# Opening two of the four PSUM results of each seven-product pair with a ScalarE copy and a VectorE sum

## The chip, the cores and the metric

The kernel runs on one core of a Trainium2 chip. The metric is the device time of one execution in microseconds (us). Engines are named as in the profile: PE is TensorE (PEld its weight loads), DVE is VectorE, ACT is ScalarE, POOL is GpSimd, SP is SyncE, which only issues DMAs here.

## The reference

A decoder of two layers on 256 positions (SEQ) of width 2048 in fp32: a mixer (attention and a gated recurrence between an input and an output projection), a SwiGLU feed-forward net (FFN), and a gated embedding per layer (PLE). The parts that the change touches are the last products of each block:

```python
mix = jnp.concatenate([attn, hgrn], axis=-1) @ w_out          # 2048 -> 2048
ffn = (jax.nn.silu(h @ w_ffn_gate) * (h @ w_ffn_up)) @ w_ffn_down   # 2048 -> 5632 -> 2048
ple = jax.nn.sigmoid(h @ w_ple_gate) * (p @ w_ple_proj)       # gate: 2048 -> 2048
```

Residuals and RMS norms lie between them (the names `mix`, `ffn`, `ple` and `h` stand in for the reference's functions).

## The kernel before

Weights stream from HBM in slabs 512 columns wide (W); one DMA of 512 KB brings 256 rows of the depth. Every fp32 weight tile `wr` is split in two: ScalarE casts the high half `wh` (L307), VectorE makes the low half `wl` = `wr` - `wh` (L317). Activations are held split and transposed in the tiles `ck`. A block product is then three matmuls into the same PSUM bank: high by high, low by high, high by low. They are L420, L423 and L424 in `paired`, and L332, L333 and L335 in `strip`, which does the columns that aren't paired. One bank holds 128 positions by 512 columns, so a strip of 512 columns needs two banks, t = 0 and t = 1.

`paired` handles two strips of 512 columns at once. Most of the depth is done plainly (`plain`): results e and a are t = 0 and 1 of the first strip (`wa`), c and d are t = 0 and 1 of the second (`wb`). On the first 512 rows of the depth (256 per block) the 2 by 2 block product is done with seven block products instead of eight (`fast`), and with `half` also on half of the next 512 rows. For this, sums of activation blocks (`sum`, from `mixed`) are made beforehand, and differences of weight blocks (`sub`, L436) on VectorE. An eighth quantity, u, is summed in a bank of another pool (tile name `ms`), in three steps:

- u's first products; they are a part of e. ScalarE copies u to SBUF (`saved`, L429; the first entry of `x`).
- after c's first products, p5 = a copy of c (L429 again); then e's and a's first products.
- `second` adds products to u and copies it again (for c, the first entry of `y`).
- `third` adds to c, adds to u a last time, copies it (for a), and adds u to p5 on VectorE (L498; that sum is for d).

At the end of each result, `summed` adds the saved tile to the bank on VectorE (L397) and hands the sum to the caller. The FFN's down projection does the addition itself: L1258 in the first group of hidden columns (bank plus saved tile into `macc`), L1260 and L1262 in the later ones (bank, then saved tile, onto `macc`).

There are 19 paired calls in a layer: two in the output projection `w_out` (the second with t = 1 running SKEW slabs behind t = 0), ten with `half` for gate and up of the FFN (a in gate's columns, c and d in up's), six in `w_ffn_down` (of which three a layer with `mixed_order`, which interleaves the strips), one in `w_ple_gate`. With two layers that is 38.

The pool `pacc` has four banks for e, a, c and d; u's pool has four too. The code calls the engines in a program order; Tile's scheduler then orders each engine's queue by its own cost model and puts the semaphore waits in. Every engine works its queue in order. Callers matter at three places: `merged` (L1187) after `w_out`, where a sum of squares (L201, ScalarE) and a product with the gain (L1187, VectorE) read each result, followed by the norm L559 and the transposes on PE (L227); `gated`, where ScalarE's L1210 (Silu) and VectorE's L1217 read results; and `gate_of` (L1302 to L1304), the PLE gate, which also ends the program.

Of the kernel before, what the change touches and what calls it, by code (L numbers as in the profile page):

```python
# [12 lines left out]
ALU = mybir.AluOpType  # L13
# [34 lines left out]
def decoder(ctx: ExitStack, tc: tile.TileContext, x, p, positions, w_in, attn_sinks,  # L48
# [16 lines left out]
    V, S, G, T = nc.vector, nc.scalar, nc.gpsimd, nc.tensor  # L65
# [29 lines left out]
    def tick():  # L95
        clock[0] += 1
        for gen in list(running):
            if next(gen, True):
                running.remove(gen)
        for item in [q for q in queue if q[0] <= clock[0]]:  # L100
            queue.remove(item)
            item[1]()

    def nat(shape=(P, W), dt=F32):
        return np_.tile(list(shape), dt, tag="nat", name="nat")

    def bank(shape=(P, W)):
        return pms.tile(list(shape), F32, tag="ms", name="ms")
# [44 lines left out]
    ps = bank()  # L153
# [49 lines left out]
    def split(src, hi, lo):  # L203

        a = S.copy(hi, src)  # L205
        v = V.tensor_tensor(lo, src, hi.bitcast(F32), op=ALU.subtract)  # L206
        return a, v
# [102 lines left out]
    def load_w(w, c, col, raw=None, hi=None):  # L310

        if raw is None:
            raw = fetch_w(w, c, col)
        if hi is None:
            hi = high(raw)
        lo = wps.tile([P, 2, W], F32R, tag="wl", name="wl")
        marks["lo"] = V.tensor_tensor(lo, raw, hi.bitcast(F32), op=ALU.subtract)  # L317
        return hi, lo
# [75 lines left out]
    def summed(done):  # L394

        def both(t, ps, x):
            V.tensor_tensor(x, ps, x, op=ALU.add)  # L397
            done(t, x)
        return both

    def paired(lhs, sums, wa, wb, cols, done_a, done_b, nch=8, row0=0, skews=(0, 0),
               after=None, mixed_order=False, half=None):

        base = row0 // (2 * P)
        opened = {}

        def psum(name):
            return pacc.tile([P, W], F32, tag="acc", name=name)

        def block(c, t):  # L410
            def get(k):
                kt = 2 * c + k
                return tuple(a[:, kt % 4, t * P:(t + 1) * P] for a in lhs[kt // 4])
            return get

        def acc(ps, x, hl, ks=(0, 1)):
            hi, lo = hl
            for k in ks:
                xh, xl = x(k)
                T.matmul(ps, xh, hi[:, k], start=id(ps) not in opened, stop=False,  # L420
                         skip_group_check=True)
                opened[id(ps)] = ps
                T.matmul(ps, xl, hi[:, k], start=False, stop=False, skip_group_check=True)  # L423
                marks["pe"] = T.matmul(ps, xh, lo[:, k], start=False, stop=k == ks[-1],  # L424
                                       skip_group_check=True)

        def saved(ps):
            b = nat()
            S.copy(b, ps)  # L429
            return b  # L430

        def parts(r):
            return load_w(None, 0, 0, raw=r)

        def sub(dst, p, q):
            V.tensor_tensor(dst, p, q, op=ALU.subtract)  # L436

        def split_one(r, k):
            hi = wps.tile([P, 2, W], F32R, tag="wh", name="wh")
            lo = wps.tile([P, 2, W], F32R, tag="wl", name="wl")  # L440
            split(r[:, k], hi[:, k], lo[:, k])
            return hi, lo

        def fast():
            mix = sums()
            r11, r12 = fetch_w(wa, base, cols[0]), fetch_w(wb, base, cols[1])
            if half:
                more = half()
                g, p = fetch_w(wa, base + 2, cols[0]), fetch_w(wb, base + 2, cols[1])
            r21, r22 = fetch_w(wa, base + 1, cols[0]), fetch_w(wb, base + 1, cols[1])  # L450
            u = bank()
            acc(u, block(0, 0), parts(r11))
            if half:
                gx = parts(g)
                acc(u, block(2, 0), gx, (0,))
            x = [saved(u)]
            sub(r11, r12, r11)
            c = psum("accc")
            acc(c, mix(1), parts(r11))
            if half:  # L460
                sub(g[:, 0], p[:, 0], g[:, 0])
                acc(c, more(1), split_one(g, 0), (0,))
            p5 = saved(c)
            tick()
            e = psum("acce")
            acc(e, block(1, 0), parts(r21))
            if half:
                acc(e, block(2, 0), gx, (1,))
            sub(r11, r22, r11)
            sub(r21, r21, r11)  # L470
            a = psum("acca")
            acc(a, block(1, 1), parts(r21))
            if half:
                sub(g[:, 0], p[:, 1], g[:, 0])
                sub(g[:, 1], g[:, 1], g[:, 0])
                g24 = parts(g)
                acc(a, block(2, 1), g24, (1,))
                sub(p[:, 0], p[:, 1], p[:, 0])
            tick()
            sub(r12, r22, r12)  # L480
            y = []

            def second():
                acc(u, mix(2), parts(r11))
                if half:
                    acc(u, more(2), g24, (0,))
                y.append(saved(u))

            def third():
                acc(c, mix(4), parts(r22))  # L490
                if half:
                    p32 = parts(p)
                    acc(c, more(4), p32, (1,))
                acc(u, mix(3), parts(r12))
                if half:
                    acc(u, more(3), p32, (0,))
                x.append(saved(u))
                V.tensor_tensor(p5, u, p5, op=ALU.add)  # L498
                y.append(p5)
                tick()  # L500
            return e, a, c, x, y, second, third

        head = 3 if half else 2

        def plain(w, col, banks, skew, end, c0=head, c1=nch, then=None):
            n = c1 - c0
            ws = {}
            for i in range(n + skew):
                if i < n:
                    ws[i] = load_w(w, base + c0 + i, col)  # L510
                    acc(banks[0], block(c0 + i, 0), ws[i])
                    if i == n - 1 and end:
                        end(0)
                if i >= skew:
                    acc(banks[1], block(c0 + i - skew, 1), ws[i - skew])
                if then and i == 0:
                    then()
                tick()
            if end:
                end(1)  # L520

        e, a, c, x1, x2, second, third = fast()

        def end_a(t):
            done_a(t, (e, a)[t], x1[t])

        def end_b(t):
            done_b(t, (c, d)[t], x2[t])
        if mixed_order:
            plain(wa, cols[0], (e, a), 0, None, c1=nch - 2, then=second)  # L530
            third()
            d = psum("accd")
            plain(wb, cols[1], (c, d), 0, None, c1=nch - 2)
            plain(wa, cols[0], (e, a), 0, end_a, c0=nch - 2)
            plain(wb, cols[1], (c, d), 0, end_b, c0=nch - 2)
            return
        def then():
            second()
            if after:
                after[0]()  # L540
        plain(wa, cols[0], (e, a), skews[0], lambda t: t or end_a(t), then=then)
        third()
        end_a(1)
        if after:
            after[1]()
        d = psum("accd")
        plain(wb, cols[1], (c, d), skews[1], end_b)

    def load_gain(g, col):
# [210 lines left out]
    for l in range(DEPTH):  # L760
# [473 lines left out]
        for gi, glen in enumerate(FF_GROUPS):  # L1234
# [11 lines left out]
            for s in range(4):  # L1246
# [5 lines left out]
                def done(t, ps, x, s=s, gB=gB if last else None):  # L1252
                    m = macc[s][:, t]
                    if gi == 0:
                        if x is None:
                            S.copy(m, ps)
                        else:
                            V.tensor_tensor(m, ps, x, op=ALU.add)  # L1258
                        return
                    V.tensor_tensor(m, ps, m, op=ALU.add)  # L1260
                    if x is not None:
                        V.tensor_tensor(m, x, m, op=ALU.add)  # L1262
                    if last:
                        square_sum(m, ssf[t][:, s:s + 1])
                        V.tensor_tensor(m, m, gB, op=ALU.mult)
                        if s == 3:
                            post_norm(macc, ssf, t, nss, nxT, gain_cols(64, l, 16), (4, 3)[t])
# [96 lines left out]
```

## Time and profile before

| | |
|---|---|
| runs of the kernel | 2342.43, 2343.69, 2344.05 us (median 2343.69) |
| profiled execution | 2343.71 us, its span 2342.0 us |
| granted TensorE clock, mean | 0.998 |
| products of 512 columns in `paired`: one group, L420 on e | x456, 177.9 us by the records, 390 ns each |
| casts L307 | x974, 1005.2 us, mean 1054 ns |
| low halves L317 | x974, 1160.1 us, mean 1222 ns |
| additions L397 on e, a, c, d | 26 each, 682 to 688 ns |
| HBM read and written | 474.57 and 29.36 MB, 215 GB/s over the span |

Matmuls are pipelined: their records overlap, and the time from start to start is what a product costs. In the lists of single instructions an entry is start, length, engine, line, operation, output and inputs, and in brackets the idle time before it and what ended it. In the groups (instructions of one line and form) come the count, the busy time, the mean, and the idle time before them.

### The profile page before, as it was taken

To read this page: it belongs to the slowest core of one execution; us is meant where nothing else is said; L and a number is where in the kernel's file an instruction comes from. 1 tells how busy PE (TensorE), PEld (TensorE's weight loads), DVE (VectorE), ACT (ScalarE), POOL (GpSimd) and SP (SyncE) were. 2 spreads that over 40 slices of the span, in tenths; PEclk is the share of its full clock that TensorE was granted. 3 is DMA by queue.
4 is the path that set the end of the run, shared out by engine and by line. 5 is a ranking of instruction groups with operands and counts; after the bars stand their busy time and mean duration, and the time that the engine had idled before them with its cause. 6 is when DMAs were issued, how large, how long until landed. Compare 5 with 4: busy or idle time off the path is not lost.

```text
span 2342.0 us, 33183 instructions
## 1 busy us (share of the span) xinstructions
PE 2326.9 (99%) x11731; PEld 1914.5 (82%) x11731; DVE 1971.1 (84%) x2535; ACT 1412.5 (60%) x2050; POOL 114.7 (5%) x229
## 2 busy tenths in 40 slices
PE   9999999999999999999999999999999999999999
PEld 7888888888888888888788888888888888888887
DVE  7786878898998999888767868788989989988885
ACT  6576557565656566657556665566656556565564
POOL 4100001000000000002010000010000000000010
PEclk9999999999999999999999999999999999999999
DMA  8666467576557565766776674676757575676743
GB/s 294 221 212 214 150 233 253 175 248 214 202 203 257 200 234 189 276 217 201 228 219 216 205 232 138 225 241 197 262 170 240 206 255 180 215 236 231 256 162 135
DMA packets 301671, 506.14 MB, mean 216 GB/s; under 512 B 23712, under 2 KB 69696, under 8 KB 301504
## 3 DMA queue, kind: packets, MB, share of 16 engines
q1 hardware_dynamic: 301200, 503.93, 64.6%
q8 instruction: 92, 1.51, 0.3%
q14 instruction: 75, 0.61, 0.1%
q0 software_dynamic: 64, 0.02, 0.0%
q10 hardware_dynamic: 240, 0.07, 0.0%
HBM read 474.57 MB, written 29.36 MB: 215 GB/s over the span
## 4 chain that ended last, share of the span: by engine, by line
PE 91%; DVE 4%; DMA 2%; issue 1%; ACT 1%; POOL 1%; SPq 0%; DVEq 0%; ACTq 0%; POOLq 0%
PE acc L332 10%; PE acc L335 10%; PE acc L333 10%; PE accc L420 5%; PE accc L423 5%; PE accc L424 5%; PE acce L420 4%; PE acca L420 4%; PE acce L423 4%; PE acca L423 4%; PE acce L424 4%; PE acca L424 4%; PE accd L424 3%; PE accd L420 3%; PE accd L423 3%; PE ms L420 3%
## 5 line engine op out<-in xcount | busy, mean ns | idle before, releaser
L307 ACT CAST wh<-wr 128x1024 fp32r<-128x1024 f32 x974 | 1005.2, 1054 | 726.5 <-DVE wr L436 208.5
L317 DVE TENSOR_TENSOR wl<-wr,wh 128x1024 fp32r<-128x1024 f32 x974 | 1160.1, 1222 | 242.3 <-ACT wh L307 230.5
L332 PE MATMUL acc<-wh,ck 128*128 128x512 f32 x1120 | 442.4, 395 | 0.7 <-ACT ck L205 0.7
L335 PE MATMUL acc<-wl,ck 128*128 128x512 f32 x1120 | 436.6, 391 | 0.8 <-DVE wl L317 0.8
L333 PE MATMUL acc<-wh,ck 128*128 128x512 f32 x1120 | 437.1, 391 | 0.1
L335 PEld LDWEIGHTS acc<-wl,ck 128*128 128x128 f32 x1120 | 210.2, 188 | 45.9 <-DVE wl L317 2.0
L332 PEld LDWEIGHTS acc<-wh,ck 128*128 128x128 f32 x1120 | 210.2, 188 | 44.0 <-ACT ck L205 0.9
L333 PEld LDWEIGHTS acc<-wh,ck 128*128 128x128 f32 x1120 | 210.4, 188 | 42.2 <-DVE ck L206 0.5
L436 DVE TENSOR_TENSOR wr<-wr 128x1024 f32<-128x1024 f32 (+1 forms) x232 | 235.5, 1039 | 1.2
L420 PE MATMUL acce<-wh,ck 128*128 128x512 f32 x456 | 177.9, 390 | 0.0
L424 PE MATMUL acce<-wl,ck 128*128 128x512 f32 x456 | 177.4, 389 | 0.0
L420 PE MATMUL acca<-wh,ck 128*128 128x512 f32 x456 | 177.4, 389 | 0.0
L423 PE MATMUL acce<-wh,ck 128*128 128x512 f32 x456 | 177.4, 389 | 0.0
L424 PE MATMUL acca<-wl,ck 128*128 128x512 f32 x456 | 177.4, 389 | 0.0
L423 PE MATMUL acca<-wh,ck 128*128 128x512 f32 x456 | 177.4, 389 | 0.0
L424 PE MATMUL accd<-wl,ck 128*128 128x512 f32 x360 | 141.6, 393 | 0.2
L420 PE MATMUL accd<-wh,ck 128*128 128x512 f32 x360 | 140.5, 390 | 0.0
L423 PE MATMUL accd<-wh,ck 128*128 128x512 f32 x360 | 140.1, 389 | 0.0
L423 PE MATMUL accc<-wh,ck 128*128 128x512 f32 x360 | 140.1, 389 | 0.0
L420 PE MATMUL accc<-wh,ck 128*128 128x512 f32 x360 | 140.0, 389 | 0.0
L424 PE MATMUL accc<-wl,ck 128*128 128x512 f32 x360 | 140.0, 389 | 0.0
L420 PEld LDWEIGHTS acce<-wh,ck 128*128 128x128 f32 x456 | 85.7, 188 | 18.0 <-ACT ck L205 0.3
(278 smaller groups left out, 3211.9 us busy)
## 6 DMA issues: line engine op xcount, KB each, us to landing
wr<-in_w_in_dram SPq DMA_DIRECT2D x176, 512.0 KB, 4.6
wr<-in_w_ffn_gate_dram SPq DMA_DIRECT2D x176, 512.0 KB, 5.9
wr<-in_w_ffn_up_dram SPq DMA_DIRECT2D x176, 512.0 KB, 6.1
wr<-in_w_ffn_down_dram SPq DMA_DIRECT2D x176, 512.0 KB, 7.3
wr<-in_w_out_dram SPq DMA_DIRECT2D x64, 512.0 KB, 5.0
wr<-in_w_ple_gate_dram SPq DMA_DIRECT2D x64, 512.0 KB, 5.0
turn<-nat SPq DMA_DIRECT2D x86, 256.0 KB, 2.5
nat<-turn SPq DMA_DIRECT2D x344, 64.0 KB, 3.6
```

The costliest lines, as they stand in the source:

```text
L307: marks["hi"] = S.copy(hi, raw)
L317: marks["lo"] = V.tensor_tensor(lo, raw, hi.bitcast(F32), op=ALU.subtract)
L332: T.matmul(ps[t], xh, hi[:, k], start=first, stop=False)
L333: T.matmul(ps[t], xl, hi[:, k], start=False, stop=False)
L335: marks[t, c] = marks["pe"] = T.matmul(ps[t], xh, lo[:, k], start=False, stop=last)
L420: T.matmul(ps, xh, hi[:, k], start=id(ps) not in opened, stop=False, skip_group_check=True)
L423: T.matmul(ps, xl, hi[:, k], start=False, stop=False, skip_group_check=True)
L424: marks["pe"] = T.matmul(ps, xh, lo[:, k], start=False, stop=k == ks[-1], skip_group_check=True)
L436: V.tensor_tensor(dst, p, q, op=ALU.subtract)
```

## The change

u's first copy goes to PSUM: ScalarE copies u into bank e (`moved`) and marks the bank as opened, so that e's first product accumulates on it. In `third`, VectorE's sum of u and p5 goes into bank d, and d's first product accumulates on that. For e and d nothing is left to add at the end, so `summed` hands the bank on, and the callers read PSUM there. a and c stay as they were. In the down projection the first group copies bank e and bank d to `macc` on ScalarE, a branch that was there for `strip`; the later groups leave L1262 out. Bank c is taken from the pool ahead of e.

```diff
     def summed(done):
         def both(t, ps, x):
+            if x is None:
+                done(t, ps)
+                return
             V.tensor_tensor(x, ps, x, op=ALU.add)
             done(t, x)
...
+        def moved(dst, src):
+            S.copy(dst, src)
+            opened[id(dst)] = dst
+            return dst
...
-            x = [saved(u)]
+            c = psum("accc")
+            e = moved(psum("acce"), u)
+            x = [None]
             sub(r11, r12, r11)
-            c = psum("accc")
             acc(c, mix(1), parts(r11))
...
             p5 = saved(c)
             tick()
-            e = psum("acce")
             acc(e, block(1, 0), parts(r21))
...
                 x.append(saved(u))
-                V.tensor_tensor(p5, u, p5, op=ALU.add)
-                y.append(p5)
+                d = psum("accd")
+                V.tensor_tensor(d, u, p5, op=ALU.add)
+                opened[id(d)] = d
+                y.append(None)
                 tick()
+                return d
...
-            third()
-            d = psum("accd")
+            d = third()
             plain(wb, cols[1], (c, d), 0, None, c1=nch - 2)
...
-        third()
+        d = third()
         end_a(1)
         if after:
             after[1]()
-        d = psum("accd")
         plain(wb, cols[1], (c, d), skews[1], end_b)
```

The lines below the edit move by up to 9: L420, L423 and L424 become L423, L426 and L427, L429 becomes L437, L397 becomes L400; the new copy is L431, and the sum L498 is now L507 with a bank as its output. The number of matmuls stays the same.

What moves in the queues shows at three places. PE, first gate/up pair, where u's third step ends (`ms`) and d begins, before:

```order
L424 MATMUL ms_4442<-wl_4646,sum_4243 128x512
L420 MATMUL accc_4463<-wh_4673,ck_3211 128x512
L423 MATMUL accc_4463<-wh_4673,ck_3212 128x512
L424 MATMUL accc_4463<-wl_4675,ck_3211 128x512
L420 MATMUL accc_4463<-wh_4673,ck_3211 128x512
L423 MATMUL accc_4463<-wh_4673,ck_3212 128x512
L424 MATMUL accc_4463<-wl_4675,ck_3211 128x512
L420 MATMUL accd_4670<-wh_4673,ck_3211 128x512
```

The same place on PE with the change:

```order
L427 MATMUL ms_4436<-wl_4638,sum_4237 128x512
L423 MATMUL accc_4454<-wh_4665,ck_3211 128x512
L426 MATMUL accc_4454<-wh_4665,ck_3212 128x512
L427 MATMUL accc_4454<-wl_4667,ck_3211 128x512
L423 MATMUL accc_4454<-wh_4665,ck_3211 128x512
L426 MATMUL accc_4454<-wh_4665,ck_3212 128x512
L427 MATMUL accc_4454<-wl_4667,ck_3211 128x512
L423 MATMUL accc_4454<-wh_4683,ck_3213 128x512
L426 MATMUL accc_4454<-wh_4683,ck_3214 128x512
L427 MATMUL accc_4454<-wl_4685,ck_3213 128x512
L423 MATMUL accc_4454<-wh_4683,ck_3213 128x512
L423 MATMUL accd_4658<-wh_4665,ck_3211 128x512
```

Between u's last product and d's first one there were six products on c, and now there are ten. In the last pair of each group of hidden columns there are seven instead of six.

ScalarE, PLE pair of layer 0, where the first copy of u was (`nat_10507`) and where p5 is copied (`nat_10521`), before:

```order
L307 CAST wh_10593<-wr_10591 128x1024
L307 CAST wh_10631<-wr_10629 128x1024
L201 ACTIVATE junk_10617,ssx0_9959<-x_9648 128x512
L1302 ACTIVATE nat_10481<-acc1_10313,rp1_10267 128x512
L307 CAST wh_10649<-wr_10647 128x1024
L307 CAST wh_10667<-wr_10665 128x1024
L307 CAST wh_10685<-wr_10683 128x1024
L201 ACTIVATE junk_10627,ssx1_9960<-x_9650 128x512
L429 COPY nat_10507<-ms_10496 128x512
L429 COPY nat_10521<-accc_10510 128x512
```

The same place on ScalarE with the change (`acce_10456` is bank e, `nat_10469` is p5):

```order
L307 CAST wh_10540<-wr_10538 128x1024
L431 COPY acce_10456<-ms_10444 128x512
L307 CAST wh_10578<-wr_10576 128x1024
L201 ACTIVATE junk_10564,ssx0_9907<-x_9596 128x512
L1311 ACTIVATE nat_10429<-acc1_10261,rp1_10215 128x512
L307 CAST wh_10596<-wr_10594 128x1024
L307 CAST wh_10614<-wr_10612 128x1024
L307 CAST wh_10632<-wr_10630 128x1024
L201 ACTIVATE junk_10574,ssx1_9908<-x_9598 128x512
L437 COPY nat_10469<-accc_10455 128x512
```

The first copy of u has moved ahead of four casts and both sums of squares; the copy of p5 has stayed behind them.

ScalarE, second pair of the output projection in layer 0, before:

```order
L201 ACTIVATE junk_3564,ssm0_3205<-nat_3309 128x512
L307 CAST wh_3691<-wr_3689 128x1024
L201 ACTIVATE junk_3574,ssm1_3206<-nat_3254 128x512
L429 COPY nat_3600<-ms_3589 128x512
L429 COPY nat_3614<-accc_3603 128x512
```

And with the change:

```order
L201 ACTIVATE junk_3562,ssm0_3205<-nat_3308 128x512
L307 CAST wh_3687<-wr_3685 128x1024
L201 ACTIVATE junk_3571,ssm1_3206<-accd_3452 128x512
L431 COPY acce_3598<-ms_3586 128x512
L307 CAST wh_3705<-wr_3703 128x1024
```

Here the copy of u has kept its place behind a cast and a sum of squares; the sum of squares before it now reads bank d of the first pair, and p5's copy has moved one cast back.

In the FFN's gate and up pairs the sum into bank d (L507) stands, as L498 did, behind the first low half of the next pair on VectorE; with the last pair of a group no low half is ahead of it.

## The prediction

> **What bounds the kernel now.** I read the shares of the page first, then the list of waits of PE, then the timeline at each place where PE stood still.
>
> ```profile
> span 2342.0 us, 33183 instructions
> ...
> PE 2326.9 (99%) x11731; PEld 1914.5 (82%) x11731; DVE 1971.1 (84%) x2535; ACT 1412.5 (60%) x2050; POOL 114.7 (5%) x229
> ```
>
> TensorE is busy all the time, and VectorE's 84% and ScalarE's 60% are no bound as such. A "busy" PE says little, so the question is how regularly its products start. Here are the last product of a partial sum u and the first product on bank d in a gate/up pair, with six products on bank c between (list of single instructions: start, length, engine, line, output and inputs):
>
> ```profile
> 449.68 0.39 PE L424 MATMUL ms<-wl,sum 128*128 128x512 f32 x1
> ...
> 451.26 0.39 PE L420 MATMUL accd<-wh,ck 128*128 128x512 f32 x1
> ```
>
> Seven starts lie 1.58 us apart, so a product costs 0.226 us although its record is 0.39 us long. The number of products doesn't change, so only stops between them, and the last few microseconds, can move the time. PE's own list of waits (total us, times, longest) is short:
>
> ```profile
> PE ms L420 <- ACT nat L429: 2.0, 1, 2.0
> PE ms L227 <- DVE x L559: 1.9, 4, 0.8
> ...
> PE acc L335 <- DVE wl L317: 0.8, 2, 0.4
> ...
> PE ms L215 <- DMA x<-in_x_dram: 0.2, 1, 0.2
> ```
>
> A weight transfer isn't in it; the one DMA is the load of x at the start. So SP's slightly changed order of loads is hidden behind PE, and I count it at nothing; one load that came too late would cost its own wait once, and there is no row to size it by. VectorE's 76 saved additions (two of four in each of 38 pairs) shorten nothing by being gone: they lie beside PE. They count only where PE waits behind one of them.
>
> **What the change removes.** Three places.
>
> (1) The PLE gate of layer 0. PE stops for a PSUM bank of u that ScalarE hasn't copied out yet:
>
> ```profile
> 1134.52 0.39 PE L332 MATMUL ms<-wh,pT 128*128 128x512 f32 x1
> 1136.94 0.79 PE L420 MATMUL ms<-wh,sum 128*128 128x512 f32 x1 [2.04 <-ACT nat L429]
> ```
> ```profile
> 1132.43 2.93 ACT L307 CAST wh<-wr 128x1024 fp32r<-128x1024 f32 x3
> 1135.70 0.63 ACT L201 ACTIVATE junk<-x 128x512 f32<-128x512 f32 x1 [0.33 <-ACT wh L307]
> ...
> 1136.33 0.57 ACT L429 COPY nat<-ms 128x512 f32<-128x512 f32 x1
> ```
>
> The copy isn't needed early, so it stands behind three casts and a sum of squares. The pitch is 2.42 us, 2.19 too long. After it PE runs at half clock (stretches: bounds, length, busy time and instructions of PE, PEld, DVE, ACT, POOL, then granted clock):
>
> ```profile
> 1134.00:1136.90 2.90, 0.90 (x4) 0.40 (x3) 2.90 (x4) 2.57 (x6) 0.00 (x0) 1.00 0.70 210
> 1136.90:1140.40 3.50, 3.46 (x8) 2.78 (x9) 2.52 (x3) 2.34 (x3) 0.00 (x0) 0.51 0.97 324
> ...
> 380.00:388.00 8.00, 6.84 (x34) 5.05 (x34) 7.19 (x15) 7.57 (x24) 3.99 (x8) 1.00 0.75 244
> ```
>
> Eight products take 3.50 us instead of 8 x 0.226 = 1.81, another 1.69. With the change, e's first product needs u's copy, and the copy stands ahead of four casts and both sums of squares in ScalarE's queue. Both go: 2.19 + 1.69 = **-3.9 us**. In layer 1 there is no such row (the list has it once).
>
> (2) The end of the output projection, once a layer:
>
> ```profile
> 381.88 0.39 PE L333 MATMUL acc<-wh,ck 128*128 128x512 f32 x1
> 383.02 0.66 PE L227 MATMUL ms<-ident,x 128*128 128x128 f32 x4 [0.76 <-DVE x L559]
> ...
> 385.36 0.40 PE L333 MATMUL acc<-wh,ck 128*128 128x512 f32 x1
> 386.16 0.50 PE L335 MATMUL acc<-wl,ck 128*128 128x512 f32 x1 [0.40 <-DVE wl L317]
> ```
> ```profile
> 378.99 0.68 DVE L397 TENSOR_TENSOR nat<-accd,nat 128x512 f32<-128x512 f32 x1
> 379.58 1.22 DVE L317 TENSOR_TENSOR wl<-wr,wh 128x1024 fp32r<-128x1024 f32 x1
> ...
> 382.21 2.75 DVE L559 SCALAR_TENSOR_TENSOR x<-mg,po,x 128x512 f32<-128x512 f32 x4 [0.81 <-POOL po L196]
> ```
>
> PE loses 1.14 - 0.23 = 0.91 and 0.80 - 0.23 = 0.57 us. The addition on d (0.59 us to the next start) falls away, ScalarE squares bank d directly, and the low half wl that stood behind it (1.13 us to the next start) now stands after the transposed copies. That is 1.7 us earlier for x, enough for the first stop; the second one waits for just such a low half, now later still, and stays. 2 x 0.91 = **-1.8 us** (ends: -3.0 if both stops go, +1.0 if the moved low halves make the second 0.5 us longer and the first only half goes).
>
> (3) The end of the program:
>
> ```profile
> 2335.77 0.39 PE L424 MATMUL accd<-wl,ck 128*128 128x512 f32 x1
> ```
> ```profile
> 2336.20 0.69 DVE L397 TENSOR_TENSOR nat<-accd,nat 128x512 f32<-128x512 f32 x1 [5.26 <-PE accd L424]
> ```
> ```profile
> 2336.92 0.91 ACT L1302 ACTIVATE nat<-nat,rp 128x256 f32<-128x256 f32 x2 [7.43 <-DVE nat L397]
> ```
>
> ScalarE can start on bank d 0.05 us after PE's end at 2336.16, not at 2336.92: **-0.7 us**. Gains: 6.4 us.
>
> **What it adds: two waits on PE in each pair.** PE's first product on e now waits for a ScalarE copy, the first one on d for a VectorE addition. Whatever stands behind it on PE waits too, and there is nothing to overtake: PE works in order. From the row at 386.16 I take how a late wait is paid: the low half ends, PE starts 0.05 us later and the next product 0.34 us after that instead of 0.23, so a stop costs (end of what is awaited) + 0.05 - (regular start) + 0.11.
>
> Neither operation is in the trace with a PSUM output. The nearest rows (groups: count, busy us, mean ns):
>
> ```profile
> L429 ACT COPY nat<-ms 128x512 f32<-128x512 f32 x114 | 65.8, 578 | 4.0 <-PE ms L424 4.0
> ...
> L498 DVE TENSOR_TENSOR nat<-ms,nat 128x512 f32<-128x512 f32 x38 | 26.1, 686 | 3.9 <-ACT nat L429 3.9
> ```
>
> Same engines, operations, sizes and source; I take 0.58 and 0.69 us. Bounds:
>
> ```profile
> L1210 ACT ACTIVATE nat<-nat,ry 128x512 f32<-128x512 f32 x40 | 28.9, 722 | 12.7 <-DVE nat L397 12.7
> ```
> ```profile
> L375 DVE TENSOR_TENSOR nat<-nat 128x256 f32<-128x256 f32 x56 | 21.4, 421 | 0.1
> ...
> L559 DVE SCALAR_TENSOR_TENSOR x<-macc,po,x 128x512 f32<-128x512 f32 x16 | 11.1, 749 | 3.1 <-POOL po L196 3.1
> ```
>
> A copy as long as L1210 is 0.14 us more, at 7 late places 1.0; an addition like L559's is 0.06 more, at some 26 places 1.6. Downward, an addition like the half-size L375 saves 0.27 each, which wipes out the gate/up stops (3.2) and halves two in the FFN, 3.7; a copy shorter by as much as L1210 is longer, 1.0.
>
> (4) Gate/up pairs, 20 of them, bank e: 9 products of u, then 9 of c, so e is due 10 x 0.227 = 2.27 us after u's last start. ScalarE needs at most one cast before the copy and ends by 1.1: no stop.
>
> (5) Gate/up, bank d. VectorE at the same place as the first rows above:
>
> ```profile
> 450.32 1.23 DVE L317 TENSOR_TENSOR wl<-wr,wh 128x1024 fp32r<-128x1024 f32 x1 [0.65 <-ACT wh L307]
> 451.47 0.69 DVE L498 TENSOR_TENSOR nat<-ms,nat 128x512 f32<-128x512 f32 x1
> ```
>
> The sum of u and p5 stands behind a low half of the next pair, and begins 1.79 us after u's last start (449.68), and ends at 2.48. Before, d began at 1.58. In the changed order ten products of c come first, so d is due at 11 x 0.227 = 2.49; 2.48 + 0.05 - 2.49 + 0.11 = 0.15 us in each of 12 pairs. In the other 8 (last of a group, seven products of c, due 1.81; the sum there ends at 1.82 as no low half is ahead) 0.17. Together 12 x 0.15 + 8 x 0.17 = **+3.2 us**. Here the sum is most sensitive: 0.1 us on VectorE moves it by 2.0.
>
> (6) Second pair of the output projection, bank e, twice:
>
> ```profile
> 332.40 1.04 ACT L307 CAST wh<-wr 128x1024 fp32r<-128x1024 f32 x1
> ...
> 333.96 0.57 ACT L429 COPY nat<-ms 128x512 f32<-128x512 f32 x1
> ```
> ```profile
> 331.94 0.39 PE L424 MATMUL ms<-wl,ck 128*128 128x512 f32 x1
> ...
> 333.52 0.39 PE L420 MATMUL acce<-wh,ck 128*128 128x512 f32 x1
> ```
>
> ScalarE's order in front of the copy stays the same (a cast, a sum of squares, the copy), without a gap to squeeze. It ends at 334.53, and e is due at 333.52: 1.01 + 0.05 + 0.11 = 1.17, **+2.3 us**.
>
> (7) FFN down pairs, bank e: in four of them the copy stands behind a cast whose buffer is u's own high half. This is how late such a cast is:
>
> ```profile
> 523.00 1.06 ACT L307 CAST wh<-wr 128x1024 fp32r<-128x1024 f32 x1 [0.56 <-PE ms L423]
> ```
> ```profile
> 522.80 0.39 PE L424 MATMUL ms<-wl,nat 128*128 128x512 f32 x1
> ```
>
> It begins 0.20 after u's last start; then the copy runs from 1.20 to 1.77, e is due at 7 x 0.227 = 1.59: 0.34 each, **+1.4 us**. Bank d in the 12 down pairs: the third u of a first pair has eight products of c in front (due 2.04). The copy there can end at 1.13, but a low half and one more VectorE row stand ahead, so the sum ends near 2.44: 0.56 x 2; the last pair of a layer 0.22 x 2; the others have 11 to 13 products in front, 0.1 or nothing: **+1.8 us** with the first output pairs (0.15 each). The PLE pair, e, layer 0: **+0.3**.
>
> **The sum.** -3.9 - 1.8 - 0.7 + 3.2 + 2.3 + 1.4 + 1.8 + 0.3 = +2.6 us on 2343.71, the profiled execution's own time (its span and 1.7 us around it; the median of the runs shown is 2343.69, so no correction). I say **2346.5**.
>
> **Rivals.** (A) *The additions are later than in (5)*: the opening sum on VectorE stands behind a low half whose cast waits on ScalarE; before, a late sum delayed nobody, now it holds d, then everything behind it. For: 12 sums end within 0.01 us of d's due time. Against: PE stopping gives both engines time. If it is 0.3 us later than I think at 20 places: +6, so 2352; from +0.1 it decides the sign.
>
> (B) *The clock falls.* The 2.04 us wait is followed by 3.50 us at 0.51; the stops of 0.76 and 0.40 us in 380 to 388 leave it at 1.00. The new one in (6), 1.06, lies between. If it is enough, twice 1.69 more: 2350.
> The Trainium skill, "TensorE: Matmul & The Clock Gate", Part 1, says that the gate goes to half only after an idle window of about 3.4 us, free-running; by that no stop here costs clock, but by that the 2.04 us one shouldn't have either, and the row decides.
>
> (C) *The waits are covered*: each pair frees VectorE for 1.2 us and a later row can move up, so that only (6) stays of the losses: 2343.7 - 6.4 + 2.3 = 2339.6, and with both stops of (2) gone 2338.4. For: PE's rows hold sums as close as 0.01 us. Against: the queues are in order, and what was removed stood behind the sums, not before them.
>
> (D) *(1) doesn't go away*: the second u of the PLE pair is refused by another late copy (p5's stands behind the same sum of squares): 2346.5 + 3.9 = 2350.4. Against: p5's bank isn't asked for until the third u.
>
> **How the numbers follow.** Forecast 0.47 (own range 2342 to 2349: the copy and addition bounds of -4.7 and +2.6 reach from 2341.8 to 2349.1), A 0.20, B 0.08, C 0.18, D 0.07. 0.2% is 4.7 us, about what a measurement of this kernel can tell from no change: faster means under 2339.0, slower over 2348.4. C lies on that edge, so faster gets 0.13; slower takes A, B, D and a small piece of the forecast, 0.37; same 0.50. The range, to hold 8 in 10: 2338 to 2353.
>
> **What would show it.** PE's list of waits gets rows "acce <- ACT" (some seven, the longest about 1.1 near 333) and "accd <- DVE" (some twenty, each under 0.2, or in PEld's list), and loses "ms <- ACT nat". The PLE stretch runs at clock 1.00. The last ScalarE row starts right after PE's end. I am wrong if d's waits are over 0.3 us, if e stops in gate/up pairs, or if the clock falls at a new place.

## The result, and the profile after

The changed kernel takes 2371.3 us (median of 4 runs, 2370.58 to 2375.21); the kernel before, run beside it, 2343.06 (2341.29 to 2344.05). The ratio is 1.0121, with a 95% interval of 1.0109 to 1.0133: slower by some 28 us, and far outside the range. Of all the executions of the experiments below one, of E2, took 5642.26 us and doesn't enter its ratio.

The page of the changed kernel, its first lines, and PE's list of waits (total us, times, longest):

```profile
span 2369.4 us, 33059 instructions
...
PE 2340.4 (99%) x11731; PEld 1917.4 (81%) x11731; DVE 1931.1 (82%) x2459; ACT 1419.1 (60%) x2054; POOL 127.0 (5%) x229
```
```profile
PE acce L423 <- ACT ck L205: 10.0, 6, 2.1
PE accc L423 <- ACT nat L437: 4.3, 2, 2.4
PE acce L426 <- DVE ck L206: 1.9, 5, 0.5
PE acce L423 <- ACT acce L431: 1.7, 2, 0.9
...
PE accd L423 <- DVE accd L507: 0.3, 1, 0.3
```

VectorE's busy time fell by 40 us, and PE's wait for the PLE copy is gone. The two waits that the change adds are rows four and five, and small. The first three rows are something else: L205 and L206 split a block of activations (`ck`), and L437 is the copy of p5.

To see where time went I took, for every product of 512 columns, the time from its start to the next start on PE, less the regular 0.2266 us, and summed that by stretches that begin with each pair's first product (so that a stretch also holds the strips behind it). The sums are in us, of the profiled executions; E1 to E6 are the experiments below.

| stretch | before | after | E1 | E2 | E3 | E4 | E5 | E6 |
|---|---|---|---|---|---|---|---|---|
| first FFN down pair (s = 0 and 1), 8 | 8.1 | 32.3 | 15.7 | 5.5 | 19.3 | 8.1 | 5.3 | 5.1 |
| later FFN down pair, 4 | 0.0 | 2.7 | 2.8 | 1.3 | 0.0 | 0.0 | 2.0 | 0.0 |
| gate/up, 20 | 0.5 | 3.3 | 3.4 | 3.4 | 0.5 | 0.5 | 0.2 | 0.5 |
| output projection, 4 | 5.7 | 5.6 | 5.7 | 5.8 | 5.7 | 2.7 | 8.4 | 2.8 |
| PLE, 2 | 9.6 | 6.3 | 6.3 | 6.3 | 7.7 | 6.5 | 6.2 | 6.0 |
| all pairs | 23.9 | 50.1 | 33.9 | 22.2 | 33.2 | 17.8 | 22.2 | 14.4 |

The sum grows by 26.2 us, nearly the whole difference of the spans (27.4), and 24.2 of it lies in one row: the first down pair of each group of hidden columns. There the pair needs the hidden block that the gate/up pair just before it has made. That block goes from VectorE (L1226, in the kernel before L1217, and the transpose L253) through DRAM (store L260, four loads L266 on SP) back to ScalarE (L205) and VectorE (L206). The rows below are of the second such pair of layer 0, first in the kernel before (PE around its first product with the new block, then ScalarE and SP; SPq is SP's queue, its time the issue), then in the changed kernel:

```profile
641.60 0.39 PE L424 MATMUL acca<-wl,ck 128*128 128x512 f32 x1
641.82 0.39 PE L420 MATMUL accd<-wh,ck 128*128 128x512 f32 x1
...
642.33 0.49 PE L420 MATMUL acce<-wh,ck 128*128 128x512 f32 x1
```
```profile
641.65 0.62 ACT L205 CAST ck<-nat 128x512 fp32r<-128x512 f32 x1 [1.52 <-DMA nat<-turn]
```
```profile
633.93 0.34 SPq L260 DMA_DIRECT2D turn<-nat  x1
635.04 0.37 SPq L301 DMA_DIRECT2D wr<-in_w_ffn_down_dram  x1
635.97 1.75 SPq L266 DMA_DIRECT2D nat<-turn  x4
```
```profile
648.22 0.39 PE L427 MATMUL acca<-wl,ck 128*128 128x512 f32 x1
650.62 0.50 PE L423 MATMUL acce<-wh,ck 128*128 128x512 f32 x1 [2.02 <-ACT ck L205]
651.35 0.51 PE L426 MATMUL acce<-wh,ck 128*128 128x512 f32 x1 [0.22 <-DVE ck L206]
```
```profile
649.95 0.62 ACT L205 CAST ck<-nat 128x512 fp32r<-128x512 f32 x1 [0.49 <-DMA nat<-turn]
650.48 0.58 ACT L437 COPY nat<-accc 128x512 f32<-128x512 f32 x1
```
```profile
638.98 0.37 SPq L301 DMA_DIRECT2D wr<-in_w_ffn_down_dram  x1
639.60 0.34 SPq L260 DMA_DIRECT2D turn<-nat  x1
640.71 1.50 SPq L301 DMA_DIRECT2D wr<-in_w_ffn_down_dram  x2
643.94 2.70 SPq L266 DMA_DIRECT2D nat<-turn  x4
```

Two things have changed. **The cover:** before, PE turned to bank d after a's product at 641.60 and had nine products of d to do, with the new block's products strewn in; now d waits for the third sum, so e's last products, which need the new block, come next, and PE stands for 2.17 us. **The block comes later:** one more weight load (638.98) stands ahead of the store on SP's queue, and the loads back start 4.34 us after the store's issue (639.60 to 643.94) instead of 2.04 (633.93 to 635.97). The trace's landing times show why: counted from the pair's first product (630.91 and 636.20), the store lands at 5.01 before and the loads back are issued at 5.02; with the change the load ahead of it lands at 7.06, the store at 7.72, and the loads back are issued at 7.74. One more weight load also stands between the store and the loads back (two at 640.71, where there was one). Counted in the same way, ScalarE's cast ends at 11.4 and 14.4, and VectorE's half at 12.1 and 15.1. The copy of p5 stands right behind the cast, and c's next products wait for it: that is the second row of PE's waits.

### The profile page after: what moved, and what is told of

The parts are those of the page before. It is cut to its first block, busy times and chain, and to the rows that moved or that the text cites. A ratio compares the mean times of both kernels' runs of the same rounds, so it can differ in the third digit from the quotient of the medians.

```text
span 2369.4 us, 33059 instructions
## 1 busy us (share of the span) xinstructions
PE 2340.4 (99%) x11731; PEld 1917.4 (81%) x11731; DVE 1931.1 (82%) x2459; ACT 1419.1 (60%) x2054; POOL 127.0 (5%) x229
## 3 DMA queue, kind: packets, MB, share of 16 engines
q8 instruction: 92, 1.51, 0.3%
## 5 line engine op out<-in xcount | busy, mean ns | idle before, releaser
L423 PE MATMUL acce<-wh,ck 128*128 128x512 f32 x456 | 180.8, 396 | 12.1 <-ACT ck L205 10.0
L426 PE MATMUL acce<-wh,ck 128*128 128x512 f32 x456 | 179.1, 393 | 1.9 <-DVE ck L206 1.9
L427 PE MATMUL acce<-wl,ck 128*128 128x512 f32 x456 | 178.7, 392 | 0.0
L423 PE MATMUL acca<-wh,ck 128*128 128x512 f32 x456 | 177.4, 389 | 0.0
L427 PE MATMUL acca<-wl,ck 128*128 128x512 f32 x456 | 177.4, 389 | 0.0
L426 PE MATMUL acca<-wh,ck 128*128 128x512 f32 x456 | 177.4, 389 | 0.0
L423 PE MATMUL accd<-wh,ck 128*128 128x512 f32 x360 | 144.3, 401 | 0.3 <-DVE accd L507 0.3
L427 PE MATMUL accd<-wl,ck 128*128 128x512 f32 x360 | 140.5, 390 | 0.0
L426 PE MATMUL accd<-wh,ck 128*128 128x512 f32 x360 | 140.4, 390 | 0.0
L426 PE MATMUL accc<-wh,ck 128*128 128x512 f32 x360 | 140.1, 389 | 0.0
L427 PE MATMUL accc<-wl,ck 128*128 128x512 f32 x360 | 140.1, 389 | 0.0
L423 PE MATMUL accc<-wh,ck 128*128 128x512 f32 x360 | 140.0, 389 | 0.0
L423 PEld LDWEIGHTS acce<-wh,ck 128*128 128x128 f32 x456 | 86.3, 189 | 35.1 <-ACT ck L205 12.5
```

## The experiments

Three theories for the 25.8 us that I then put down to these places (some 1.5 us of it are the first stops of the pairs behind them, as the table shows): the late block alone (L), the lost cover alone (C), or both together (B). E1 to E3 complete the square of block on time or late, covered or not; E4 to E6 try the two parts of the change apart and by place.

**E1: the loads behind the store.** The changed kernel, with SP's order at these places as before.

```diff
+    stores, held = [], {}
     def fetch_w(w, c, col):
         raw = wpr.tile([P, 2, W], F32, tag="wr", name="wr")
-        nc.sync.dma_start(raw, ...)
+        n = held["n"] = held.get("n", 99) + 1
+        with tc.issue_after(stores[-2 if n == 11 else -1].ins) if 11 <= n <= 13 else nullcontext():
+            nc.sync.dma_start(raw, ...)
         return raw
```

`stores` holds the stores L260; `held["n"]` is set to 0 ahead of each first down pair.

> The changed kernel, with two or three weight loads of each first FFN down pair (s = 0 and 1) put back behind the store of the last hidden block on SP's queue, as it was before. Three theories for the 25.8 us that the eight such pairs lose. L: the last hidden block comes 2.6 us later, since its store to DRAM now stands behind one more weight load; that alone costs 2 to 4 us a pair. C: d's twelve early products, which ran while the block was on its way, now wait for the third sum, and that alone costs it. B: each is hidden unless the other is there too. L: about 2346 (2371.3 less 25.8). C: 2371, as the cover is still gone. B: 2346 to 2350 (PE asks for the block 12.2 us into the pair; its high half would be there at 11.8, its low half at 12.5: 0 to 0.5 us a pair).

Measured: 2353.18 us, ratio 1.0039 (1.0025 to 1.0054); the first down pairs hold 15.7 us. In the same pair as above ScalarE's cast now ends 11.1 and VectorE's half 12.5 us after its first product. So SP's order is worth 18 us in a kernel without the cover, 16.6 of it in these pairs. The edit sets three loads back (one from ahead of the first store to behind it, two from there to behind the second store), so it doesn't tell the load ahead of the store from the one behind it. But 9 of the 25.8 us stay, more than B's 0 to 0.5 a pair: PE is now held by low halves of both kinds, of the block (L206, at 644.91) and of the weights, and in two pairs by the copy of p5 (2.8 us in PE's list).

```profile
644.61 0.39 PE L427 MATMUL acce<-wh,ck 128*128 128x512 f32 x1
644.91 0.50 PE L430 MATMUL acce<-wh,ck 128*128 128x512 f32 x1
646.04 0.50 PE L431 MATMUL acce<-wl,ck 128*128 128x512 f32 x1 [0.63 <-DVE wl L321]
```

**E2: bank d as before in the first down pairs.** Everywhere else as in the change (the flag is set in the call for `w_ffn_down`).

```diff
-                V.tensor_tensor(d, u, p5, op=ALU.add)
-                opened[id(d)] = d
-                y.append(None)
+                if open_d:
+                    ...
+                else:
+                    V.tensor_tensor(p5, u, p5, op=ALU.add)
+                    y.append(p5)
...
+                           open_d=s > 1)
```

> The changed kernel, but bank d of the eight first FFN down pairs is opened as before (u plus p5 saved and added at the end), so d's twelve products stand ahead of the third step again. SP's order stays that of the change: the block's store is still behind one more load. L: 2371, since the block is still late. C: 2345.5 (2371.3 less 25.8). B: 2345.5 to 2348: twelve products are 2.7 us, so PE asks for the block at 14.9 us, when its low half is ready at 14.7 to 15.1.

Measured: 2342.54 us, ratio 0.9995 (0.9986 to 1.0005). SP's order is still that of the change, and the block is about as late (cast 13.8 to 15.2 us after the pair's first product, against 13.8 to 14.4):

```profile
644.55 0.39 PE L427 MATMUL acca<-wl,ck 128*128 128x512 f32 x1
644.78 0.39 PE L423 MATMUL accd<-wh,ck 128*128 128x512 f32 x1
...
647.27 0.39 PE L427 MATMUL accd<-wl,ck 128*128 128x512 f32 x1
647.50 0.39 PE L423 MATMUL acce<-wh,ck 128*128 128x512 f32 x1
```
```profile
645.74 0.62 ACT L205 CAST ck<-nat 128x512 fp32r<-128x512 f32 x1
646.26 0.58 ACT L437 COPY nat<-accc 128x512 f32<-128x512 f32 x1
```

Twelve products of d run from 644.78 to 647.50; the cast ends at 646.36 and the copy of p5 at 646.84, and no stop is left. L is refuted: a late block that is covered costs nothing. The time is even 3 us below what C and B gave, since these pairs stop less than before the change (5.5 against 8.1). E2 also shows that the load's move isn't due to the down pair's own bank d. E4 to E6 have SP's order of before: E5 opens e everywhere and d nowhere, E4 d only in the second output pairs and the PLE pairs. So the move comes with d in one of the other pairs, most likely in the gate/up pairs just ahead, which no run opened alone.

**E3: the kernel before, with d opened by the sum in the first down pairs only.** The same flag; SP's order is that of before.

> The kernel before, but bank d of the eight first FFN down pairs is opened by the VectorE sum: the cover is gone, and SP's order is that of before. L: 2343 to 2344. C: about 2369 (2343.1 plus 25.8). B: 2343 to 2350: PE asks for the block 10.9 us into the pair, and the high half ends between 9.9 and 11.4 there, the copy of p5 behind it 0.6 to 1.2 later: 0 to 0.9 us a pair.

Measured: 2353.58 us, ratio 1.004 (1.0025 to 1.0055). The block is on time (cast 10.0 to 11.2, VectorE's half 12.1 us after the pair's first product, as before), and still the pairs lose 11.2 us more than before: 1.0 to 2.1 each.

```profile
642.81 0.39 PE L427 MATMUL acca<-wl,ck 128*128 128x512 f32 x1
643.43 0.50 PE L423 MATMUL acce<-wh,ck 128*128 128x512 f32 x1 [0.23 <-ACT ck L205]
644.29 0.50 PE L426 MATMUL acce<-wh,ck 128*128 128x512 f32 x1 [0.35 <-DVE ck L206]
```

C's 2369 and L's 2344 both fail, and so does B as it was put, "each is hidden unless the other is there too": its range (to 2350) counted the cast and p5's copy and left out VectorE's half (4.6 us of PE's waits) and a copy of u that stands behind the cast too (PE waits 4.5 us in 3 places for such copies, with the PLE one). Only half of B is left: the late block costs nothing while it is covered. In these pairs the lost cover alone costs 8 to 11 us (E1 and E3 less before), the late block alone nothing (E2), and both together 24. Some 5.6 of the 24 are a fall of the clock (see the last section), of which E1 and E3 show nothing there (mean granted clock 1.000 in both).

**E4: opened only where it gains.** e in the PLE pairs, d in the second output pairs and the PLE pairs. The first line goes into the calls for gate and up and for `w_ffn_down`, the second into that for `w_out`.

```diff
+               open_e=False, open_d=False)
...
+               open_e=False, open_d=s == 2)
```

> e opened by the copy in the PLE pairs alone, d opened by the sum in the second output pair and the PLE pairs alone; all else as before. All theories: PE's stop in the first PLE pair goes (measured 3.6 with the half clock), the stops at the end of the output projection shrink (1.4 a layer), and 0.7 at the program's end, so about 2336.5.

Measured: 2336.84 us, ratio 0.9969 (0.9956 to 0.9982), as expected.

**E5: e alone.** The change without its part on d.

```diff
-                d = psum("accd")
-                V.tensor_tensor(d, u, p5, op=ALU.add)
-                opened[id(d)] = d
-                y.append(None)
+                V.tensor_tensor(p5, u, p5, op=ALU.add)
+                y.append(p5)
```

> The changed kernel with bank e opened by the copy as there, and bank d as before. SP's order at the first down pairs is then that of before, and seven of d's products stand ahead of the third step, five behind it. If both the loss of cover and the late block come from opening d (C, L and B alike), nothing of the 25.8 us is left. From the changed kernel's own stops: 3.6 less in the PLE pair, 2.3 more in the second output pairs, 1.4 more in the later down pairs, 0.3 in the second PLE pair: 2343.9 plus 0.4, so about 2344; 2 less if the first down pairs lose their small stops as they did without d. A theory by which opening e does the harm gives 2365 or more.

Measured: 2342.06 us, ratio 0.9993 (0.9984 to 1.0003). The loss is d's part alone. The output projection shows both its terms apart here: 8.4 against 5.7 us, so e costs 2.7 there (the second pair 2.4 of it), and in the changed kernel d takes 2.8 off again. The first down pairs lose less than before the change.

**E6: both, by place.** e in the first down pairs and the PLE pair of layer 0; d in the second output pairs and the PLE pairs.

> Opened by the copy: bank e in the eight first down pairs and the PLE pair of layer 0. Opened by the sum: bank d in the second output pair and the PLE pairs. All else as before. From the run that opened e in PLE and d in the second output and PLE pairs (2336.8): 0.3 less, since e of layer 1's PLE pair goes back, and up to 2.9 less, if the first down pairs lose their small stops as in the run with d old there: 2333.6 to 2336.5. If e's copy there costs a stop of its own (0.35 as in the later down pairs), 2339.

Measured: 2333.60 us, ratio 0.996 (0.9948 to 0.9972): 10 us under the kernel before and 38 under the changed one. Against E4, e's stop in layer 1's PLE pair is gone (0.3 us), and the first down pairs fall from 8.1 to 5.1 us.

## Why the prediction was wrong

Most steps that it worked out came out near; what it lacked was a step. (Its terms add up to 2346.3, where it says 2346.5.)

**Right.** (1): PE's stop in the PLE pair and the half clock behind it are gone, and e's own stop there is 0.28 us; the PLE row falls by 3.3 (forecast -3.9 + 0.3). (3): ScalarE starts 0.04 us after PE's end at 2364.22:

```profile
2363.83 0.39 PE L427 MATMUL accd<-wl,ck 128*128 128x512 f32 x1
```
```profile
2364.26 0.84 ACT L1311 ACTIVATE nat<-accd,rp 128x256 f32<-128x256 f32 x2 [6.71 <-PE accd L427]
```

(4): e in gate/up pairs doesn't stop. (5): the sum ends 2.44 us after u's last product, d starts at 2.50, and the next product is 0.11 late; 2.8 us for 20 pairs (forecast 3.2).

```profile
451.36 0.39 PE L427 MATMUL ms<-wl,sum 128*128 128x512 f32 x1
...
453.86 0.50 PE L423 MATMUL accd<-wh,ck 128*128 128x512 f32 x1
454.19 0.40 PE L426 MATMUL accd<-wh,ck 128*128 128x512 f32 x1
```

(6): the copy stands where it was said to, and the stop is 336.72 - 335.46 - 0.23 = 1.03, and 0.11 on the next product: 1.14 (forecast 1.17), without a fall of the clock.

```profile
335.46 0.39 PE L427 MATMUL accc<-wl,sum 128*128 128x512 f32 x1
336.72 0.50 PE L423 MATMUL acce<-wh,ck 128*128 128x512 f32 x1 [0.87 <-ACT acce L431]
```

The operations with PSUM outputs cost what their neighbours do: 579 ns for the copy (0.58 taken), 694 for the sum (0.69 taken).

**Mis-sized.** (2): both stops at the end of the output projection went, where the second was said to stay (E4's row is 2.7, with no stop over 0.25 us): about 2.9 us instead of 1.8, the end that the range held. (7), later down pairs: e's stop is 0.35 as said, but d stops too, 0.24 in each of four, where "0.1 or nothing" was taken: 2.7 instead of 1.4 and a little.

**Wrong: (7), bank d in the first down pairs, and "SP's slightly changed order of loads is hidden behind PE, and I count it at nothing".** Step (7) asked when the sum would be ready for d's first product, and priced that. It didn't ask what PE would do in the place that d's products had held: they ran ahead of the third step and were the cover for the hidden block's way through DRAM. And the load that moved past the store was dismissed because PE's list had no wait for a weight load; what it delayed was the small store behind it. The late store alone cost nothing (E2), the lost cover alone 11 us in these pairs (E3); together they cost 24, and the forecast for these pairs was 1.6. Rival (A) named the additions, which weren't late; (B)'s fall of the clock did happen, but at the new stops, not at (6). (C) and (D) weren't it either.

What stays open: why the scheduler put that load ahead of the store. SP's rows show that it did, and E2, E4 and E5 that d's opening in earlier pairs brings it about; its reason wasn't tried. How much of the lateness comes from the load ahead of the store and how much from the one between it and the loads back wasn't separated, nor how much of E1's remaining 9 us is the lost cover and how much the weights' low halves.

## What to carry to other kernels

An accumulation that may start on an empty bank is also filler: an engine that works in order can do it while something else is on its way. Before a bank is given an initial value, look for what waits behind its products, and price the wait that they cover, not only the new one. And a small transfer in a chain counts by what stands ahead of it on its queue: a reordered load costs nothing itself and may still delay the store that PE needs 10 us later.

## What the runs showed of the hardware

A 256 KB store that was issued 0.62 us behind a 512 KB load had its loads back start 4.34 us later; with no load just ahead, 2.04. Over the eight pairs it is 4.1 to 4.4 in the changed kernel and 2.0 to 2.1 in the kernel before; with the load put behind the store (E1) it is 2.1 to 2.9.

Whether PE's clock falls behind a stop isn't told by the stop's length. Stretches of the changed kernel at four first down pairs (bounds, length, busy time and instructions by engine, then the granted clock); the first and the last row begin with stops of 2.17 and 2.23 us, the second with one of 1.63, and the third with the longest of all, 2.51:

```profile
648.40:655.10 6.70, 4.45 (x12) 3.11 (x12) 3.78 (x4) 2.63 (x4) 0.00 (x0) 0.75 0.90 258
840.90:844.20 3.30, 1.40 (x5) 0.67 (x4) 3.30 (x4) 2.57 (x4) 0.00 (x0) 1.00 0.93 298
1693.90:1697.00 3.10, 0.75 (x4) 0.34 (x3) 3.00 (x4) 2.58 (x4) 0.00 (x0) 1.00 0.86 315
...
2205.60:2211.60 6.00, 3.93 (x10) 2.44 (x10) 4.00 (x4) 2.63 (x4) 0.00 (x0) 0.72 0.86 280
```

The clock fell in four of the eight pairs, once behind a stop of only 1.74 us (with 0.60 right behind it), for some 28 products at 0.2 us extra each: about 5.6 of the 24 us. What the stop's length leaves open, its place tells in part. The trace's clock records have the half clock begin at 522.00, 651.71, 1825.89 and 2208.18 us, each time for 3.41 us, and these times lie 38, 344 and 112 times 3.413 us apart. In the 3.41 us just ahead of each of them PE was busy for 1.16 to 1.51 us. In three of the pairs without a fall the lowest stretch on the same grid has 1.95 to 1.98; the stop of 2.51 lies across a bound of the grid (1696.18), with 1.50 busy in the stretch ahead of it, so that the busy time alone doesn't settle this one.

The Trainium skill, "TensorE: Matmul & The Clock Gate", Part 1, has the activity window running freely, so that the phase counts; the rows agree with that, and not with its figure of about 3.4 us of idle time, since every stop here is shorter.
